# One decoder layer, one NeuronCore: token blocks of 264, or of 512, 512 and 32, instead of 352 in the merge's gate products

## The chip, the cores and the metric

The kernel runs on one core of a Trainium2 chip. The metric is the device time of one launch in microseconds. A core has TensorE (PE in the profile; PEld is its loading of weights), VectorE (DVE), ScalarE (ACT), GpSimd (POOL) and SyncE (SP, which only issues DMAs here). Each engine runs its own list of instructions in order, and waits on semaphores for the others.

## The reference, cut to what matters

One decoder layer for 1024 prompt tokens and 8 samples of 4 tokens, 1056 columns of 1024 features, all in float32:

```
u = x * (1 + scale1) + shift1
z = u @ w_in + b_in        # -> lru_in | lru_gate | s5_in | merge_gate_A | merge_gate_B, 1024 each
A = (RG-LRU(conv(lru_in)) * gelu(lru_gate)) @ w_lru_out
B = GLU(gelu(S5(s5_in)))   # 64 groups of 16 channels, a complex state of 64 each
mix = (sigmoid(merge_gate_A) * A + sigmoid(merge_gate_B) * B) @ w_out
x = LN(alpha * x + gate1 * mix);  x = LN(alpha * x + gate2 * SwiGLU(...))
```

The change is in the products for merge_gate_A and merge_gate_B, the last 2048 columns of w_in.

## The kernel before, in words

Features lie on the 128 partitions, tokens along the free dimension. A product takes one weight tile (1024 x 128, eight k tiles) against all 1056 tokens, and its tokens go in three blocks of 352, each into one of eight PSUM banks that are handed out in turn (`bank`). Weights and activations are each split into a high and a low part in float32r; a block is 8 k tiles x 3 combinations (high x high, high x low, low x high) = 24 matmuls of 128x128 weights on 352 columns, with a weight load for each (`mm`, L328). ACT makes the high part of the next weight tile (L216) and POOL the low part (L108) while the present one is used. The activations of w_in's products lie in `r1`: high or low, token block, k tile, 352 tokens. `make_u` writes them at the start.

The program is written out in one order for every engine. Each token block begins with a `tick`, and the S5's steps are noted against ticks (`S5_PLAN`, `s5_batch`), so that they land between blocks. The S5 goes in eight batches of groups, a new one every six ticks, which is two weight tiles of three blocks. Its steps on PE are the kernels (`s5_pe1`, L696), the transposes (`s5_pre4`, L706), the second stage, what each chunk adds to the states (`s5_pe2`, L734), and, for the batch before, the outputs (`s5_pe3`, L797 and L798), which need states that four DMAs copied (L784). They take 1, 2, 3 and 3 banks. DVE computes powers and rotations (L108), scans (L760) and gelu (L117), where the second gelu step (`s5_gelu2`) is the last reader of the outputs' banks. ACT copies results out of PSUM (L698 kernels, L708 transposes, L737 second stage, L800 squares of the outputs), takes the tanh for gelu (L807), prepares the scan's operands (L753, L755), and evacuates the products.

After the products of s5_in come 14 tiles for the merge's gates, eight for gate A and six for gate B, three ticks each; two more of gate B are done later, in the LRU stage. Their evacuation (L847) is a tanh on ACT into one staging buffer in the SBUF, which a DMA writes to DRAM when the tile is complete; the next tile's first evacuation waits for that DMA. Then the LRU stage begins.

Of the kernel before, what the change touches and what calls it, by code (L numbers as in the profile page):

```python
# [9 lines left out]
FT = mybir.dt.float32  # L10
# [5 lines left out]
T = 1056  # L16
# [10 lines left out]
# small operands, packed per partition: name, free shape  # L27
# [20 lines left out]
# float32 per partition  # L48
# [4 lines left out]
def _shaped(ap, shape):  # L53
    """[128, n] as [128, *shape]"""
    if len(shape) == 1:
        return ap
    names = "abcde"[:len(shape)]
    return ap.rearrange("p (" + " ".join(names) + ") -> p " + " ".join(names),
                        **dict(zip(names[1:], shape[1:])))
# [3 lines left out]
def tile_hawk_s5(ctx: ExitStack, tc: tile.TileContext, io):  # L63
# [3 lines left out]
    class Region:  # L67
        """a part of the SBUF; float32r where products read it"""
# [104 lines left out]
    r1r, r1f = acts(r1)  # L173
# [58 lines left out]
    # w_down's last part goes where the blocks of tokens have been read, one after another  # L232
# [34 lines left out]
    # w_out, and w_down's last part, stay whole: they go through the blocks of tokens  # L267
# [28 lines left out]
    def split_to(n):  # L296
        """splits of the tiles before the n-th, as far as the loads have come"""
# [14 lines left out]
    def use_w(name, m):  # L312
        """the next tile; the one after it is split meanwhile"""
# [9 lines left out]
    def mm(out, w, x, nb, kts, first=True, last=True):  # L323
        """out (+)= (hi + lo)^T (hi + lo) over k tiles, but for lo^T lo"""
# [14 lines left out]
    # =================== conditioning ===================  # L339
# [18 lines left out]
    # 2 silu(c)  # L358
# [19 lines left out]
    def ada_job():  # L378
        """two k tiles for four more tiles of the conditioning, beside the products, in the last bank"""
# [33 lines left out]
    # =================== S5 ===================  # L413
    s5m = {}

    def s5_open():
        """the S5's operands: in the right part, with the left part's help"""
# [35 lines left out]
    # exact exponentials, sines and cosines of small operands  # L453
    class Ops:
        """operations of DVE, noted down to run between others"""
# [7 lines left out]
        def turns(self, other):  # L463
            """the operations of both by turns"""
# [65 lines left out]
    def s5_small():  # L530
        """softplus(-lambda); the steps and abar, for pairs of groups and for rows of both parts"""
# [69 lines left out]
    def s5_powers():  # L601
        """abar^0..8; rows [re; im] and [-im; re]"""
# [30 lines left out]
    def s5_const1(b):  # L633
        """b abar^s and c abar^l, rows of real and of imaginary parts"""
# [30 lines left out]
    def s5_turn(ee, n0, n1):  # L665
        """e^{8 i theta (c + 1)} of the chunks c, by doubling"""
# [11 lines left out]
    def s5_turn0():  # L678
        """the first chunks, of all groups"""
# [10 lines left out]
    def s5_pe1(b):  # L690
        """the kernels c abar^l b, blocks of a Toeplitz matrix"""
# [8 lines left out]
    def s5_pre4(b):  # L700
        """b abar^s transposed"""
# [24 lines left out]
    def s5_pe2(b):  # L726
        """what each chunk adds to the states"""
# [11 lines left out]
    def s5_rot_in(b):  # L739
        """into the frame that turns with the states, where the recurrence is real"""  # L740
# [47 lines left out]
    def s5_pe3(b):  # L788
        """outputs, 2 gelu(y)"""
# [35 lines left out]
    def s5_last():  # L825
        """last states of the samples: abar^4 x0 + what the steps add"""
# [25 lines left out]
    # =================== program: z_s5, the merge's gates, S5 ===================  # L852
# [64 lines left out]
    for j in range(8):  # L917
        product(use_w("in", 24 + j), r1r, merge_evac(d_ta, j, 24 + j))
    for j in range(6):
        product(use_w("in", 32 + j), r1r, merge_evac(d_tb, j, 32 + j))  # L920

    # =================== program: LRU ===================
# [16 lines left out]
    # v, split, is kept where the last k tile goes  # L939
# [61 lines left out]
    def lru_0(j):  # L1001
        # t_c = tanh(log_a / 2), t_e = 1 + exp(log_a)
# [5 lines left out]
    def lru_1(j):  # L1008
        # t_d = 2 (1 + a) by a step of Newton's
# [561 lines left out]
```

## Time and profile before

| | |
|---|---|
| median of the 2 runs shown | 1877.1 us (1876.12 and 1878.08) |
| span of the profiled execution | 1876.2 us; the profile gives no other time of its own |
| PE busy | 1766.6 us (94%), 11640 matmuls |
| DVE busy | 974.8 us (52%) |
| ACT, POOL busy | 619.9 us (33%), 798.3 us (43%) |
| mean granted TensorE clock | 0.976 of full |

The gates' products run between about 156 and 385 us of the span. Busy shares of the whole span say little about that stretch: in its first two thirds DVE has hardly a gap, later PE has none. So it is read by stretches, and by what each engine waits for there. Times in the rows are microseconds from the span's start, then the duration; "x24" counts instructions, and brackets hold the idle time of the engine before a row with what ended it. Matmuls are pipelined, so a row of them ends with the last one's own duration.

### The profile page before, as it was taken

To read this page: it belongs to the slowest core of one execution; us is meant where nothing else is said; L and a number is where in the kernel's file an instruction comes from. 1 tells how busy PE (TensorE), PEld (TensorE's weight loads), DVE (VectorE), ACT (ScalarE), POOL (GpSimd) and SP (SyncE) were. 2 spreads that over 40 slices of the span, in tenths; PEclk is the share of its full clock that TensorE was granted. 3 is DMA by queue.
4 is the path that set the end of the run, shared out by engine and by line. 5 is a ranking of instruction groups with operands and counts; after the bars stand their busy time and mean duration, and the time that the engine had idled before them with its cause. 6 is when DMAs were issued, how large, how long until landed. Compare 5 with 4: busy or idle time off the path is not lost.

```text
span 1876.2 us, 28961 instructions
## 1 busy us (share of the span) xinstructions
PE 1766.6 (94%) x11640; PEld 1724.6 (92%) x11640; DVE 974.8 (52%) x1560; ACT 619.9 (33%) x1212; POOL 798.3 (43%) x663
## 2 busy tenths in 40 slices
PE   6899989899898899999999799999999999999994
PEld 5899988899788899999999799999999999999984
DVE  6989999648888743333248841231132112211297
ACT  4433333345554633212224552112211221122233
POOL 3557666427666622233342543223323332233435
PEclk9999999999899899999999999999999999999997
DMA  9334544431111158533351010111111111111111
GB/s 342 108 106 135 161 146 140 130 123 60 48 41 59 48 139 246 172 123 126 137 198 65 23 45 26 43 58 49 35 51 57 46 37 43 57 46 43 51 35 67
DMA packets 89846, 171.92 MB, mean 92 GB/s; under 512 B 18928, under 2 KB 54000, under 8 KB 89712
## 3 DMA queue, kind: packets, MB, share of 16 engines
q1 hardware_dynamic: 89712, 170.07, 28.1%
q8 instruction: 91, 1.49, 0.3%
q14 instruction: 43, 0.35, 0.1%
HBM read 136.86 MB, written 29.02 MB: 88 GB/s over the span
## 4 chain that ended last, share of the span: by engine, by line
PE 60%; DVE 19%; POOL 8%; issue 8%; ACT 3%; DMA 2%; SPq 0%; POOLq 0%; ACTq 0%; DVEq 0%
PE ps L328 57%; DVE s_t L108 8%; DVE norm_t L108 2%; POOL weights_t L108 2%; POOL lru_t L108 2%; DVE m_t L108 2%; POOL r_t L108 2%; DVE left_t L108 2%; DVE s_t L760 1%; DVE m_t L117 1%; PE ps L387 1%; DVE s_t L117 1%; POOL m_t L108 1%; DVE small_r_t L472 1%; DVE small_l_t L472 0%
## 5 line engine op out<-in xcount | busy, mean ns | idle before, releaser
L328 PE MATMUL ps<-r_t,weights_t 128*128 128x352 f32 x7632 | 1262.3, 326 | 2.2 <-ACT weights_t L216 1.1
L328 PEld LDWEIGHTS ps<-r_t,weights_t 128*128 128x128 f32 x7632 | 1236.7, 191 | 15.5 <-issue 8.9
L108 POOL TENSOR_TENSOR weights_t<-small_t,weights_t 128x512 fp32r<-128x512 f32 (+2 forms) x260 | 344.0, 1341 | 598.3 <-ACT weights_t L216 542.0
L216 ACT ACTIVATE weights_t<-small_t 128x512 fp32r<-128x512 f32 (+2 forms) x262 | 145.7, 599 | 257.1 <-PE ps L328 137.1
L328 PE MATMUL ps<-f_t,weights_t 128*128 128x352 f32 x1206 | 194.5, 322 | 0.0
L328 PEld LDWEIGHTS ps<-f_t,weights_t 128*128 128x128 f32 x1206 | 193.7, 188 | 0.0
L117 DVE SCALAR_TENSOR_TENSOR norm_t<-norm_t,ps 128x352 f32<-128x352 f32 x66 | 34.4, 521 | 222.4 <-ACT norm_t L1344 222.4
L108 DVE TENSOR_TENSOR s_t<-s_t 128x128 f32<-128x128 f32 (+3 forms) x200 | 134.4, 719 | 12.7 <-ACT s_t L737 7.0
L108 DVE TENSOR_TENSOR norm_t<-norm_t,ps 128x352 f32<-128x352 f32 x66 | 34.4, 521 | 195.8 <-PE ps L328 195.6
L117 DVE SCALAR_TENSOR_TENSOR m_t<-ps,small_t,m_t 128x352 f32<-128x352 f32 (+1 forms) x120 | 68.4, 570 | 126.9 <-PE ps L328 126.8
L108 POOL TENSOR_TENSOR f_t<-norm_t,f_t 128x352 fp32r<-128x352 f32 x66 | 62.7, 951 | 154.0 <-ACT f_t L1352 154.0
L117 DVE SCALAR_TENSOR_TENSOR glu_t<-glu_t,ps 128x352 f32<-128x352 f32 x48 | 24.2, 518 | 185.3 <-PE ps L328 126.3
L328 PE MATMUL ps<-r_t,f_t 128*128 128x352 f32 x648 | 107.1, 326 | 0.1
L328 PEld LDWEIGHTS ps<-r_t,f_t 128*128 128x128 f32 x648 | 105.0, 190 | 1.6 <-issue 0.5
L1352 ACT ACTIVATE f_t<-norm_t 128x352 fp32r<-128x352 f32 x66 | 32.8, 498 | 200.9 <-DVE norm_t L108 200.9
L117 DVE SCALAR_TENSOR_TENSOR lru_t<-lru_t 128x1056 f32<-128x1056 f32 (+1 forms) x52 | 81.9, 1574 | 30.6 <-ACT lru_t L998 16.6
L108 POOL TENSOR_TENSOR m_t<-m_t,norm_t 128x352 f32<-128x352 f32 x58 | 62.4, 1101 | 76.7 <-ACT norm_t L1206 64.8
L117 DVE SCALAR_TENSOR_TENSOR lru_t<-lru_t,small_t 128x352 f32<-128x352 f32 (+2 forms) x96 | 87.9, 916 | 3.4
L1344 ACT ACTIVATE norm_t<-ps 128x352 f32<-128x352 f32 x66 | 30.6, 464 | 177.1 <-PE ps L328 177.1
L108 POOL TENSOR_TENSOR left_t<-s_t 128x512 f32<-128x512 f32 (+1 forms) x40 | 77.0, 1947 | 5.8 <-DVE s_t L108 3.5
L328 PE MATMUL ps<-f_t,r_t 128*128 128x352 f32 x378 | 63.7, 327 | 0.9 <-POOL r_t L108 0.5
L328 PEld LDWEIGHTS ps<-f_t,r_t 128*128 128x128 f32 x378 | 61.0, 188 | 2.7 <-POOL r_t L108 0.8
(210 smaller groups left out, 1586.4 us busy)
## 6 DMA issues: line engine op xcount, KB each, us to landing
small_t<-in_w_up_dram SPq DMA_DIRECT2D x44, 512.0 KB
small_t<-in_w_in_dram SPq DMA_DIRECT2D x40, 512.0 KB
small_t<-in_w_ada_dram SPq DMA_DIRECT2D x32, 512.0 KB
ada_w_t<-in_w_ada_dram SPq DMA_DIRECT2D x16, 512.0 KB
small_t<-in_w_glu_dram SPq DMA_DIRECT2D x16, 512.0 KB
small_t<-in_w_down_dram SPq DMA_DIRECT2D x16, 384.0 KB
small_t<-in_w_down_dram SPq DMA_DIRECT2D x16, 320.0 KB
d_u<-left_t SPq DMA_DIRECT2D x64, 72.0 KB
```

Source lines behind the costliest of these rows:

```text
L108: e.tensor_tensor(out, a, b, op=op)
L117: e.scalar_tensor_tensor(out, a, s, b, op0=op0, op1=op1)
L216: A.activation(self.hi[:, s], self.raw[:, s], AF.Copy)
L328: PE.matmul(out[:, :NB], a[:, k, :], x[:, h, nb, k, :], start=bool(first and n == 0 and q == 0), stop=bool(last and n == len(kts) - 1 and ...
L387: PE.matmul(b[32 * j:32 * j + 32, :128], silu_c[:, 2 * i + k, :], w.raw[:, k, 128 * j:128 * j + 128], start=i == k == 0, stop=i == 3 and k ...
L472: getattr(V, name)(*a, **k)
L760: V.tensor_tensor_scan(wf[:, 512 * r:512 * r + 512], tv[:, :512], vv[:, r].rearrange("p n c -> p (n c)"), 0.0, op0=OP.mult, op1=OP.add)
L1344: A.activation(p, b[:, :NB], AF.Tanh, scale=0.5)
L1352: A.activation(frr[:, 0, nb, k, :], p, AF.Copy)
```

## The change

The two groups of gate products use a new helper, `product_wide`: the eight tiles of gate A go in four blocks of 264 tokens, the six tiles of gate B in blocks of 512, 512 and 32. Each tile keeps three ticks; a fourth block follows the third without one. So that a block may begin anywhere, `r1` now holds the tokens of a k tile as one row of 1056 (high or low, k tile, token); the other products see the same memory as three blocks of 352. The evacuation `merge_wide` takes any width. Comments and doc strings are gone from the changed file, and its lines have other numbers: L350 is the matmul of `product_wide`; L713, L723, L751, L814 and L815 are the former L696, L706, L734, L797 and L798; L330 is the former L328.

```diff
-    r1r, r1f = acts(r1)
+    r1r, r1f = (r1.v(0, 2, 8, 3, NB, t=t).rearrange("p h k n t -> p h n k t") for t in (FR, FT))
+    r1w = r1.v(0, 2, 8, T, t=FR)
...
+    def product_wide(w, x, widths, evac):
+        o = 0
+        for i, n in enumerate(widths):
+            if i < 3:
+                tick()
+            b = bank()
+            for k in range(8):
+                for q, (a, h) in enumerate(((w.hi, 0), (w.hi, 1), (w.lo, 0))):
+                    PE.matmul(b[:, :n], a[:, k, :], x[:, h, k, o:o + n], start=k == q == 0,
+                              stop=k == 7 and q == 2)
+            evac(o, n, b)
+            o += n
+        assert o == T
...
+    def merge_wide(d, j, m):
+        st = s5m["stage"]
+        def evac(o, n, b):
+            A.activation(st[:, o:o + n], b[:, :n], AF.Tanh, bias=bh[:, m - 24:m - 23], scale=0.5)
+            if o + n == T:
+                SP.dma_start(d[j], st)
+        return evac
...
     for j in range(8):
-        product(use_w("in", 24 + j), r1r, merge_evac(d_ta, j, 24 + j))
+        product_wide(use_w("in", 24 + j), r1w, (264,) * 4, merge_wide(d_ta, j, 24 + j))
     for j in range(6):
-        product(use_w("in", 32 + j), r1r, merge_evac(d_tb, j, 32 + j))
+        product_wide(use_w("in", 32 + j), r1w, (512, 512, 32), merge_wide(d_tb, j, 32 + j))
```

PE's list in a round of the S5 that falls on two tiles of gate A, from the kernels (L696, then L713) to the second stage (L734, then L751), with the semaphores that it waits for; r_t is r1. Before:

```order
L696 MATMUL ps<-s_t 32x128 [waits DVE_49,Activation_49]
L696 MATMUL ps<-s_t 32x128 x7
L328 MATMUL ps<-r_t,weights_t 128x352 [waits Activation_49]
L328 MATMUL ps<-r_t,weights_t 128x352 x23
L706 MATMUL ps<-small_t,s_t 128x128 [waits DVE_49,Pool_49]
L706 MATMUL ps<-small_t,s_t 128x128 x3
L706 MATMUL ps<-small_t,s_t 128x128 [waits DVE_49]
L706 MATMUL ps<-small_t,s_t 128x128 x3
L328 MATMUL ps<-r_t,weights_t 128x352 [waits DVE_49]
L328 MATMUL ps<-r_t,weights_t 128x352 x23
L734 MATMUL ps<-s_t 64x136 [waits DMAHW4_49,Activation_49]
```

The same round in the changed kernel:

```order
L713 MATMUL ps<-s_t 32x128 [waits DVE_49,Activation_49]
L713 MATMUL ps<-s_t 32x128 x7
L350 MATMUL ps<-r_t,weights_t 128x264 [waits DVE_49]
L350 MATMUL ps<-r_t,weights_t 128x264 x23
L723 MATMUL ps<-small_t,s_t 128x128 [waits DVE_49,Pool_49]
L723 MATMUL ps<-small_t,s_t 128x128 x3
L723 MATMUL ps<-small_t,s_t 128x128 [waits DVE_49]
L723 MATMUL ps<-small_t,s_t 128x128 x3
L350 MATMUL ps<-r_t,weights_t 128x264 [waits Activation_49]
L350 MATMUL ps<-r_t,weights_t 128x264 x23
...
L751 MATMUL ps<-s_t 64x136 [waits DMAHW4_49,Activation_49]
```

Two blocks instead of one stand between the transposes and the second stage. The block behind the kernels now waits for DVE, where it waited for ACT: it takes the first bank that the outputs of the batch before left, the one that the transposes took.

PE's list from the last batch's second stage to the first product of the LRU stage. Before:

```order
L734 MATMUL ps<-left_t,s_t 64x136 x16
L328 MATMUL ps<-r_t,weights_t 128x352 x24
L797 MATMUL ps<-s_t 128x136
L798 MATMUL ps<-s_t 128x136
...
L328 MATMUL ps<-r_t,weights_t 128x352 x144
L797 MATMUL ps<-left_t,s_t 128x136
L798 MATMUL ps<-s_t,left_t 128x136
...
L328 MATMUL ps<-r_t,weights_t 128x352 x192
```

And in the changed kernel:

```order
L751 MATMUL ps<-left_t,s_t 64x136 x16
L350 MATMUL ps<-r_t,weights_t 128x512 x24
...
L350 MATMUL ps<-r_t,weights_t 128x512 x24
L350 MATMUL ps<-r_t,weights_t 128x32 x24
L350 MATMUL ps<-r_t,weights_t 128x512 x48
L350 MATMUL ps<-r_t,weights_t 128x32 x24
L350 MATMUL ps<-r_t,weights_t 128x512 x24
L814 MATMUL ps<-left_t,s_t 128x136
...
L350 MATMUL ps<-r_t,weights_t 128x512 x24
L350 MATMUL ps<-r_t,weights_t 128x32 x24
L330 MATMUL ps<-r_t,weights_t 128x352 x144
```

One block stands between second stage and outputs of the batch before, as earlier; behind these, the six blocks of 352 have become four of 512 and two of 32. Of the 192 matmuls behind the last outputs, 48 were the gates'; they are now one block of 512 and one of 32.

## Rows read from the trace of the kernel before

**Rows 1.** The page, its first line.
```profile
span 1876.2 us, 28961 instructions
```

**Rows 2.** Windows: stretch, length, busy us per engine (instructions), granted clock, DMA.
```profile
280.00:348.50 68.50, 61.67 (x469) 59.25 (x467) 66.21 (x86) 23.71 (x61) 43.73 (x25) 1.00 0.45 140
348.50:371.40 22.90, 22.90 (x146) 22.90 (x146) 10.92 (x14) 9.05 (x22) 8.51 (x7) 1.00 0.40 112
```

**Rows 3.** Chain of waits, 90 to 420 us: shares by line; pieces (start, length).
```profile
by line: DVE s_t L108 38.8%; PE ps L328 20.4%; issue 9.8%; DVE s_t L760 6.9%; DVE left_t L108 6.8%; DVE s_t L117 4.1%; DMA s_t<-s_t 2.7%; PE ps L734 2.4%; PE ps L798 1.7%; PE ps L797 1.5%; ACT lru_t L998 0.9%; ACT s_t L684 0.5%; POOL left_t
...
345.01 0.23 PE ps L797 x2
...
364.18 2.44 DMA s_t<-s_t
...
371.29 2.45 DMA s_t<-s_t
```

**Rows 4.** Timeline of PE: a round of the S5 (start, length, line).
```profile
291.77 0.65 PE L696 MATMUL ps<-s_t 128*32 128x128 f32 x16
292.35 4.08 PE L328 MATMUL ps<-r_t,weights_t 128*128 128x352 f32 x24
297.69 1.07 PE L706 MATMUL ps<-small_t,s_t 128*128 128x128 f32 x8 [1.26 <-DVE s_t L117]
298.51 4.07 PE L328 MATMUL ps<-r_t,weights_t 128*128 128x352 f32 x24
304.72 2.10 PE L734 MATMUL ps<-s_t 128*64 128x136 f32 x32 [2.15 <-ACT s_t L708]
306.75 4.08 PE L328 MATMUL ps<-r_t,weights_t 128*128 128x352 f32 x24
...
314.29 11.70 PE L328 MATMUL ps<-r_t,weights_t 128*128 128x352 f32 x72
...
338.89 2.10 PE L734 MATMUL ps<-left_t,s_t 128*64 128x136 f32 x32 [2.13 <-ACT s_t L708]
```

**Rows 5.** Timeline of DVE in that round.
```profile
296.99 1.38 DVE L117 SCALAR_TENSOR_TENSOR s_t<-s_t,ps 128x408 f32<-128x408 f32 x3
...
303.50 6.92 DVE L108 TENSOR_TENSOR s_t<-s_t 128x64 f32<-128x64 f32 x18 [0.47 <-ACT s_t L684]
...
311.88 5.04 DVE L108 TENSOR_TENSOR s_t<-s_t 128x128 f32<-128x128 f32 x3
```

**Rows 6.** Timeline of ACT, that round and the end of the S5.
```profile
304.07 1.08 ACT L708 ACTIVATE s_t<-ps 128x512 f32<-128x512 f32 x2
...
306.50 1.23 ACT L737 ACTIVATE s_t<-ps 128x408 f32<-128x408 f32 x3
...
352.63 0.55 ACT L847 ACTIVATE left_t<-ps,small_t 128x352 f32<-128x352 f32 x1 [2.03 <-PE ps L328]
```

**Rows 7.** Timeline of PE, end of the S5.
```profile
348.46 23.14 PE L328 MATMUL ps<-r_t,weights_t 128*128 128x352 f32 x144
...
373.87 0.47 PE L798 MATMUL ps<-s_t,left_t 128*128 128x136 f32 x2 [1.57 <-DMA s_t<-s_t]
...
376.87 31.18 PE L328 MATMUL ps<-r_t,weights_t 128*128 128x352 f32 x192
```

**Rows 8.** Instructions on the banks: duration ns min/median/max, first and last start.
```profile
L328 PEld LDWEIGHTS ps<-r_t,weights_t x7632: 186/188/338, 15.5 to 1769.1; 128*128 128x128 f32 x196
L328 PE MATMUL ps<-r_t,weights_t x7632: 317/322/663, 15.5 to 1769.3; 128*128 128x352 f32 x196
...
L734 PEld LDWEIGHTS ps<-s_t x128: 133/137/230, 104.5 to 306.4; 128*64 128x64 f32 x128
```

**Rows 9.** Timeline of DVE: the last batch's scan.
```profile
355.23 2.34 DVE L760 TENSOR_TENSOR_SCAN s_t<-s_t 128x512 f32<-128x512 f32 x2 [2.65 <-POOL s_t L756]
```

**Rows 10.** Timeline of PE behind a longer wait, and that stretch's window.
```profile
167.94 3.90 PE L734 MATMUL ps<-s_t 128*64 128x136 f32 x32 [3.06 <-ACT s_t L708]
...
164.00:174.00 10.00, 6.94 (x46) 6.29 (x45) 9.30 (x23) 5.09 (x13) 3.88 (x3) 0.66 0.44 105
```

## The prediction

> **What bounds the kernel now.** I read the span first, then the busy time of each engine by stretch, then the chain of waits, and then the rows of PE, DVE and ACT through two rounds of the S5. The profiled execution spans 1876.2 us [rows 1], which is 0.9 below the median of the two runs shown, 1877.1. My sum is made against the span, and those 0.9 are added at the end.
>
> The stretch in which the gates' products run has two bounds, one after the other. From 280 to 348.5 us DVE is busy for 66.2 of 68.5 us and PE for 61.7; from 348.5 to 371.4 PE is busy all of the time and DVE for under half of it [rows 2]. The chain of waits from 90 to 420 us says the same: its largest share is DVE's S5 work and the products (L328) have 20% [rows 3]. The reader is to see that TensorE time added before about 340 us may be free, and that added later is not.
>
> In the first part a round of S5 (one batch of groups, two weight tiles) takes 34.2 us, from the second stage's matmuls at 304.72 to the next batch's at 338.89 [rows 4]. PE waits twice in it: 1.3 us before the transposes, for a DVE instruction that reads the bank they want, and 2.1 us before the second stage, for ACT's copy of the transposes. Both follow DVE's pace: DVE's second gelu instruction frees its first bank at 296.99 + 0.46 = 297.45, and its 18 rotations begin at 303.50 [rows 5], after which ACT copies the transposes from 304.07 to 305.15 [rows 6].
>
> **What one product costs.** Six blocks of 352, 144 matmuls, run without a gap from 348.46 for 23.14 us at full granted clock [rows 2, 7]; less the last one's own 0.32 [rows 8] that is 22.82 us for 143, 159.6 ns each. That clock is the 2.4 GHz level, so 352 columns are 146.7 ns and 12.9 ns are left over per matmul. A block of 24 is 3.83 us. I take the 12.9 as fixed, because each matmul brings one weight load whatever its width:
> - 264 columns: 110 + 12.9 = 122.9 ns, 2.95 us a block. A tile is 4 x 2.95 = 11.8 us against 3 x 3.83 = 11.5, 0.3 more.
> - 512 columns: 213.3 + 12.9 = 226.2 ns, 5.43 us a block. From below, the S5's f32 matmuls of 136 columns run at 0.23 us a pair [rows 3]; if a column takes them two cycles, that is 115 ns against 113.3, an excess near 2 ns, and makes 5.2. From above, in proportion to the columns, 159.6 x 512 / 352 = 232 ns makes 5.57. The middle is nearest, since it has the same operands and the same loads.
> - 32 columns: 13 ns of columns, so the load sets the pace. Loads of 128 columns last 188 ns and of 64 columns 137 [rows 8]; 51 / 64 = 0.8 ns a column, 102 ns for 128. The S5's pairs, each with its own load of 128, show that one in 115 ns can be kept. I take 110, 2.64 us a block. The upper end is 159.6, 3.83 us, as if narrowing saved nothing.
>
> A tile of 512, 512, 32 then costs 13.5 us against 11.5, 2.0 more, and six of them 12. The question is how much of it DVE's bound hides.
>
> **The eight tiles of 264.** They add 2 x 0.3 = 0.6 us to a round of two tiles. A round's PE work is now 6 x 3.83 = 23.0, plus kernels 0.57, transposes 0.82, second stage 2.03 and outputs 3.7 (314.29 - 306.75 less a block) [rows 4]: 30.1 of 34.2 us. It becomes 30.7, so 3.5 us stay idle. One order changes: with four blocks the eight banks come round one block sooner, and it is the block behind the kernels, not the transposes, that now waits for DVE's gelu. From 297.45 follow that block 2.95, transposes 0.82 and two blocks 5.9, which puts the second stage at 307.1 instead of 304.72. ACT's copies of its result ended 3.0 us after its start, at 307.73 [rows 6]; they now end near 310.1. DVE comes to its first possible reader of them at 311.88 [rows 5]. There are 1.8 us to spare, so DVE's pace stays and I cost these tiles at nothing. If that cover went, each round would be late by what is missing, next on DVE's rotations and then on ACT's queue.
>
> **The six tiles of 512, 512, 32.** They begin one block before the kernels at 291.77. From the gelu's release at 297.45 PE no longer waits. Up to the last batch's second stage come five blocks of 512 (27.15), three of 32 (7.92), twice the transposes (1.64), second stage 2.03, outputs 3.7 and kernels 0.57: 43.0 us, so 340.5 instead of 338.89, or **+1.6**. (ACT's copy, the old bound there, would have allowed about 339.2.) Behind it, before the last outputs, seven blocks of 352 (26.8) become five of 512 and two of 32 (32.4): **+5.6**. PE's wait of 1.57 us in the last outputs, for states that arrive by DMA at 373.7 [rows 3, 7], is eaten: **-1.6**. Those states will be later too, since ACT takes the second block's copy (352.63, on PE's end) ahead of the tanh and the scan's operands [rows 6], and DVE waits 2.65 us for these [rows 9]; that block ends about 4.3 us later. So the states land near 378, when PE arrives at 378.5, and they cost nothing more. The last two blocks, 7.66, become 8.07: **+0.4**. In all +6.0.
>
> The LRU stage opens on these products, and PE is on the path until it starts (192 matmuls in one run from 376.87 [rows 7]), so I expect the whole shift to stay. The order of k tile and token block in r1 changes no operand's count: ACT and POOL write the same 1056 elements per k tile, PE reads 352 contiguous columns as before. Eight more ACT evacuations and 0.15 us more for a wide one lie in ACT's slack. I cost these at nothing; if ACT were late, the states' copy and with it the rotations would be late.
>
> **Forecast**, 60%: 1876.2 + 6.0 + 0.9 = 1883. Its bounds: with blocks of 5.2 and 2.45 us, the eleven wide ones since 297.45 give back 2.5 and the six narrow ones 1.1, 1879.5; with 5.57 and 3.83 they add 1.5 and 7.1, 1892.
>
> **Rivals.**
> - The clock falls in the narrow blocks (20%), slower. PE streams for only 13 of 110 ns there, 2.6 us on end, in two of the six tiles right behind transposes of 0.8. After a wait of 3.06 us the clock went to the 1.2 GHz level: the second stage took 3.90 us instead of 2.10, and the granted clock was 0.66 over 10 us [rows 10]. That is 6.8 us at half, 3.4 us lost. The waits of 2.15 us brought no fall [rows 2, 4], and no row has a load-bound stream. All six narrow blocks lie on PE's path: one fall each makes 6.0 + 20.4, 1903.5; half of them 1893. It decides from about three falls on. The Trainium skill ("TensorE: Matmul & The Clock Gate", HAM oscillation) says that gaps in matmul work re-throttle the clock; whether a stream bound by loads counts as a gap, it does not say.
> - The narrow block costs next to nothing (8%). If 24 of them took 0.6 us, PE would be back at ACT's bound at 339, the seven blocks would be 28.4, and the last two 6.0 instead of 7.66; the states, late by the second block, would hold the last outputs by 3: about +1.4, 1878.5. Against it stand the loads' 102 to 115 ns. The Trainium skill (same page, Back-to-back issue gap) gives an issue floor of about 25 ns for 1 to 64 columns, by which this rival would come true; its section on LDWEIGHTS has 107 ns for 128 columns, and the trace agrees with that one.
> - The bank wait reaches DVE (7%), slower: where the clock falls in the 3.5 us that PE idles before the gelu's release, the second stage comes 3.4 us later than I have it, 1.6 more than the cover. Over four rounds that is +6, 1889.
> - The LRU stage takes the shift up (5%): 1877 to 1879. For that something other than PE would have to set when it starts; the rows show PE running into it without a gap [rows 7].
>
> So the range is 1876 to 1896; it leaves out the clock's worst third and mishaps on either side. Two per cent, 37.5 us, is about what a measurement of this kernel can tell from no change. No case here saves that much: the columns are the same and the loads not fewer, 1%. Slower by that would need the falling clock together with a late DVE, 3%. Within, 96%.
>
> **What would show it.** In the changed profile: matmuls of 512 columns at 226 ns and of 32 at 110; rounds of 34.2 us through the tiles of 264, with PE waiting some 3.5 us ahead of the block behind the kernels and DVE as busy as before; the last second stage near 340.5, the last outputs near 378.5 without a wait, and LRU's first product 6 us later. Wrong would be a granted clock under 1 between 300 and 390 us, narrow blocks well off 2.6 us, or rounds longer than 34.2.

## The result, and the profile after

The changed kernel takes 1886.46 us (median of 1884.69 and 1888.23) against 1877.1, a ratio of 1.0054, interval 1.0036 to 1.0072. The forecast was 1883.0, the range 1876 to 1896. Its profiled execution took 1888.23 us, 1.8 more than its span, where the forecast had put 0.9 around the span of before; with the same 1.8, the profiled execution of before was the slower of the two shown, 1878.08. In what follows a "fall" is a stretch that the record of TensorE's clock has at the 1.2 GHz level (a granted clock of about 0.5 in a window).

The page's first line, to be held against [rows 1]:

```profile
span 1886.4 us, 29354 instructions
```

The windows of the changed kernel, with the columns of [rows 2] (stretch, length, busy us of PE, PEld, DVE, ACT and POOL, granted clock, DMA):

```profile
280.00:348.50 68.50, 68.16 (x453) 59.16 (x453) 61.97 (x86) 24.41 (x61) 43.17 (x25) 0.95 0.47 139
348.50:384.00 35.50, 35.50 (x189) 30.43 (x188) 12.14 (x15) 9.49 (x22) 10.45 (x8) 0.95 0.38 108
339.50:342.70 3.20, 3.20 (x35) 3.17 (x34) 2.79 (x10) 1.40 (x5) 0.00 (x0) 1.00 0.44 81
342.70:346.10 3.40, 3.40 (x29) 3.04 (x26) 0.00 (x0) 2.30 (x5) 2.49 (x2) 0.51 0.76 161
```

Two things differ from [rows 2]. PE is busy for 68.2 of 68.5 us before 348.5 where it was busy for 61.7, and DVE has gone from 66.2 to 62.0: the bound has passed to PE some 40 us earlier than before (PE's last wait there ends at 296.37, in the rows below, and at 338.89 in [rows 4]). And the mean clock is 0.95 where it was 1.00. The last two rows show why: through a narrow block and up to its end (339.5 to 342.7) the clock is full, and in the 3.4 us behind it half. The chain of waits from 90 to 420 us says the same of the bound: products of the new form (L350) lead it, where DVE's L108 led in [rows 3].

```profile
by line: PE ps L350 29.9%; DVE s_t L108 25.0%; PE ps L330 14.1%; issue 6.0%; DVE left_t L108 5.2%; DVE s_t L777 4.6%; PE ps L751 3.8%; DVE s_t L117 3.1%; PE ps L815 2.8%; PE ps L814 2.8%; PE ps L723 1.1%; PE ps L713 0.7%; ACT s_t L701 0.3%;
```

PE's timeline, with the columns of [rows 4] (L713, L723 and L751 are the kernels, the transposes and the second stage, L696, L706 and L734 before; outputs are left out):

```profile
193.41 5.65 PE L350 MATMUL ps<-r_t,weights_t 128*128 128x264 f32 x24 [4.48 <-DVE s_t L117]
...
205.89 2.07 PE L751 MATMUL ps<-left_t,s_t 128*64 128x136 f32 x32
...
262.39 3.20 PE L350 MATMUL ps<-r_t,weights_t 128*128 128x264 f32 x24 [2.98 <-DVE s_t L117]
...
296.37 5.84 PE L350 MATMUL ps<-r_t,weights_t 128*128 128x512 f32 x24 [0.34 <-DVE s_t L117]
302.05 1.04 PE L723 MATMUL ps<-small_t,s_t 128*128 128x128 f32 x8
302.84 2.83 PE L350 MATMUL ps<-r_t,weights_t 128*128 128x32 f32 x24
305.60 2.07 PE L751 MATMUL ps<-s_t 128*64 128x136 f32 x32
307.61 5.83 PE L350 MATMUL ps<-r_t,weights_t 128*128 128x512 f32 x24
...
316.89 15.61 PE L350 MATMUL ps<-r_t,weights_t 128*128 128x512 f32 x72
...
339.48 2.83 PE L350 MATMUL ps<-r_t,weights_t 128*128 128x32 f32 x24
342.24 3.46 PE L751 MATMUL ps<-left_t,s_t 128*64 128x136 f32 x32
345.63 6.06 PE L350 MATMUL ps<-r_t,weights_t 128*128 128x512 f32 x24
...
355.15 29.40 PE L350 MATMUL ps<-r_t,weights_t 128*128 128x512 f32 x144
...
388.01 8.39 PE L350 MATMUL ps<-r_t,weights_t 128*128 128x512 f32 x48
```

At 193.41 and 262.39 PE waits 4.48 and 2.98 us ahead of the block behind the kernels, for the bank that DVE's gelu still reads, as forecast for the tiles of 264; behind the 0.34 us at 296.37 it waits for nothing. The second stage takes 2.07 us at 305.60 and 3.46 at 342.24, right behind a narrow block. From the latter to the last outputs at 384.4 stand 42.2 us, where before it was 32.5 (338.89 to 371.4). Some 1.7 us of that are only moved: 2624 tokens of the products stand in this time where 2464 did, and so many fewer behind it (24 x 160 x 0.444 ns, the pace found in e7); and in the last outputs there is no longer the wait of 1.57 us [rows 7]. Falls begin at 325.7, 342.7, 363.2 and 397.4 us and last 3.4 us each. Each begins within 1.3 us of the start of a narrow block's last matmul (325.0, 342.0, 363.3 and 396.1), so at the ends of four of the six narrow blocks. PE stood idle ahead of none of them. An earlier one, from 192.6 on for 6.8 us, begins in the wait of 4.48 us. The late second stage behind it (205.89) held DVE, whose timeline shows two waits there:

```profile
208.70 3.94 DVE L108 TENSOR_TENSOR s_t<-s_t 128x512 f32<-128x512 f32 x2 [2.00 <-ACT s_t L754]
214.86 4.48 DVE L108 TENSOR_TENSOR s_t<-left_t,s_t 128x1152 f32<-128x1152 f32 x2 [2.22 <-PE ps L815]
```

The pace, as the median from start to start in this trace: 112 ns for 32 tokens, 121 for 264, 160 for 352 and 232 for 512.

The shift against the trace of before is +13.0 us at the last outputs (371.4 to 384.4), +12.9 at the first matmul of the LRU stage's gates (412.5 to 425.4) and +10.2 at the end. From that matmul to the end the run of before took 1463.7 us and the ten profiled runs of the changed kernel (two) and of e1 to e5, e7, e9 and e10 below 1459.2 to 1462.2, so the missing 2.7 us seem to be that one run's (1878.08 us, where the same kernel's median beside e8 is 1875.66) and nothing that the LRU stage took up; in that later pairing the medians differ by 11.3.

### The profile page after: what moved, and what is told of

It is laid out like the page before. It is cut to its first block, busy times and chain, and to the rows that moved or that the text cites. A ratio compares the mean times of both kernels' runs of the same rounds, so it can differ in the third digit from the quotient of the medians.

```text
span 1886.4 us, 29354 instructions
## 1 busy us (share of the span) xinstructions
PE 1784.5 (95%) x11832; PEld 1731.3 (92%) x11832; DVE 968.0 (51%) x1560; ACT 623.6 (33%) x1220; POOL 800.1 (42%) x663
## 4 chain that ended last, share of the span: by engine, by line
PE 67%; DVE 14%; POOL 7%; issue 6%; ACT 3%; DMA 2%; SPq 1%; POOLq 0%; ACTq 0%; DVEq 0%
PE ps L330 58%; PE ps L350 5%; DVE s_t L108 5%; POOL weights_t L108 2%; DVE norm_t L108 2%; POOL lru_t L108 2%; POOL r_t L108 2%; DVE m_t L108 1%; DVE left_t L108 1%; DMA x_in_t<-in_x_dram 1%; DVE s_t L777 1%; PE ps L404 1%; DVE m_t L117 1%; PE ps L751 1%; DMA ada_w_t<-in_w_ada_dram 1%
## 5 line engine op out<-in xcount | busy, mean ns | idle before, releaser
L330 PE MATMUL ps<-r_t,weights_t 128*128 128x352 f32 x6624 | 1093.7, 326 | 1.9 <-ACT weights_t L218 1.1
L330 PEld LDWEIGHTS ps<-r_t,weights_t 128*128 128x128 f32 x6624 | 1074.7, 191 | 12.4 <-issue 6.7
L108 POOL TENSOR_TENSOR weights_t<-small_t,weights_t 128x512 fp32r<-128x512 f32 (+2 forms) x260 | 343.9, 1341 | 609.8 <-ACT weights_t L218 581.4
L350 PE MATMUL ps<-r_t,weights_t 128*128 128x264 f32 (+2 forms) x1200 | 188.4, 316 | 9.1 <-DVE s_t L117 9.1
L330 PE MATMUL ps<-f_t,weights_t 128*128 128x352 f32 x1206 | 194.5, 322 | 0.0
L330 PEld LDWEIGHTS ps<-f_t,weights_t 128*128 128x128 f32 x1206 | 193.8, 188 | 0.0
L350 PEld LDWEIGHTS ps<-r_t,weights_t 128*128 128x128 f32 x1200 | 169.2, 194 | 24.7 <-DVE s_t L117 10.2
L108 DVE TENSOR_TENSOR s_t<-s_t 128x128 f32<-128x128 f32 (+3 forms) x200 | 127.0, 683 | 17.6 <-ACT s_t L754 11.9
L108 DVE TENSOR_TENSOR norm_t<-norm_t,ps 128x352 f32<-128x352 f32 x66 | 34.4, 521 | 195.2 <-PE ps L330 195.0
L117 DVE SCALAR_TENSOR_TENSOR m_t<-ps,small_t,m_t 128x352 f32<-128x352 f32 (+1 forms) x120 | 68.4, 570 | 126.9 <-PE ps L330 126.8
L108 POOL TENSOR_TENSOR f_t<-norm_t,f_t 128x352 fp32r<-128x352 f32 x66 | 62.8, 951 | 153.3 <-ACT f_t L1378 153.3
L330 PE MATMUL ps<-r_t,f_t 128*128 128x352 f32 x648 | 106.5, 325 | 0.0
L330 PEld LDWEIGHTS ps<-r_t,f_t 128*128 128x128 f32 x648 | 104.7, 190 | 1.1 <-issue 0.5
L108 POOL TENSOR_TENSOR m_t<-m_t,norm_t 128x352 f32<-128x352 f32 x58 | 62.2, 1097 | 76.1 <-ACT norm_t L1232 65.0
L108 POOL TENSOR_TENSOR left_t<-s_t 128x512 f32<-128x512 f32 (+1 forms) x40 | 78.8, 1991 | 4.5 <-DVE s_t L777 2.3
```

Of the source, the lines that this page charges most:

```text
L108: e.tensor_tensor(out, a, b, op=op)
L117: e.scalar_tensor_tensor(out, a, s, b, op0=op0, op1=op1)
L330: PE.matmul(out[:, :NB], a[:, k, :], x[:, h, nb, k, :], start=bool(first and n == 0 and q == 0), stop=bool(last and n == len(kts) - 1 and ...
L350: PE.matmul(b[:, :n], a[:, k, :], x[:, h, k, o:o + n], start=k == q == 0, stop=k == 7 and q == 2)
```

## The experiments

My theory was: a narrow block costs the loads of 24 weights, and its end the falling clock; the first rival was that something else of the change (the 264 tiles, the layout, the 512 blocks, their evacuation) has a part in it. The kernel before ran again beside each group of these runs, with medians from 1875.27 to 1876.21 us, and each ratio is to the median beside it. The table gathers what they gave. "r6 to outputs" is the time in the profiled run from the second stage of round 6 (305.6 us in the changed kernel) to the last round's outputs (384.4), and the falls are those within it. Where gate B's blocks are 512 or 480 wide, 160 or 128 more tokens stand in that time and so many fewer behind it; these 1.7 or 1.4 us are no loss. In e3 they and one fall make most of the 3.7 us over the kernel before, and at the end nothing is lost.

| kernel | gate A | gate B | us | ratio [interval] | r6 to outputs, falls |
|---|---|---|---|---|---|
| before | 3 x 352 | 3 x 352 | 1877.1 | | 66.7, 0 |
| e1 | 4 x 264 | 3 x 352 | 1874.67 | 0.9990 [0.9982, 0.9999] | 67.1, 0 |
| e2 | 3 x 352 | 512, 512, 32 | 1886.16 | 1.0053 [1.0039, 1.0066] | 75.7, 1 |
| e3 | 4 x 264 | 512, 272, 272 | 1875.05 | 0.9992 [0.9984, 1.0001] | 70.4, 1 |
| e4 | 4 x 264 | 512, 512, 32 spread | 1882.14 | 1.0037 [1.0023, 1.0050] | 74.1, 0 |
| e5 | 3 x 352 | 3 x 352, new layout | 1875.87 | 1.0003 [0.9994, 1.0012] | 68.4, 2 |
| e8 | 4 x 264 | 512, 512, 32 (the change) | 1886.94 | 1.0062 [1.0050, 1.0075] | 78.9, 3 |
| e9 | 4 x 264 | 512, 512, 32 filled | 1881.73 | 1.0033 [1.0021, 1.0046] | 74.1, 0 |
| e10 | 4 x 264 | 480, 480, 96 | 1878.54 | 1.0018 [1.0009, 1.0027] | 71.1, 0 |
| e6 | 512, 512, 32 | 4 x 264 | 1891.70 | 1.0088 [1.0074, 1.0101] | |
| e11 | 512, 512, 32 filled | 4 x 264 | 1883.19 | 1.0041 [1.0028, 1.0053] | |
| e12 | as e11, banks moved on | 4 x 264 | 1878.03 | 1.0007 [0.9998, 1.0016] | |

### e1, e2: each gate's part alone

```diff
 e1: gate B as before, gate A as in the change
-        product_wide(use_w("in", 32 + j), r1w, (512, 512, 32), merge_wide(d_tb, j, 32 + j))
+        product(use_w("in", 32 + j), r1r, merge_evac(d_tb, j, 32 + j))
 e2: gate A as before, gate B as in the change
-        product_wide(use_w("in", 24 + j), r1w, (264,) * 4, merge_wide(d_ta, j, 24 + j))
+        product(use_w("in", 24 + j), r1r, merge_evac(d_ta, j, 24 + j))
```

> Gate A's eight tiles in four blocks of 264, gate B's six in three of 352 as before. Theory (DVE sets the pace of the S5's rounds, so PE time there is free): rounds of 34.2 us, LRU's first product within 1 us of before, total 1877 (1875.5 to 1878.5). Rival (the four blocks' bank wait, with a falling clock, reaches DVE and is part of the 9.4 us): last second stage 2 us or more later than 338.9, total 1880 or more.

> Gate A's tiles in blocks of 352 as before, gate B's in 512, 512 and 32. Theory (the whole loss comes from gate B's tiles): total 1885 to 1888, four or so falls of the granted clock between 300 and 400 us. Rival (264 is a part of it): 1880 to 1884.

The tiles of 264 alone cost nothing (1874.67). Gate B's alone give the loss: 1886.16 is 10.0 over the kernel before, and the interval overlaps with that of the changed kernel again (e8, 11.3 over). Some four falls were expected; the profile of e2, its quickest run with 1881.23 us, shows a single one, behind the narrow block that ends at 338.6:

```profile
338.50:342.50 4.00, 4.00 (x35) 3.61 (x35) 3.93 (x7) 2.51 (x6) 2.81 (x2) 0.57 0.40 75
```

```profile
335.88 2.83 PE L350 MATMUL ps<-r_t,weights_t 128*128 128x32 f32 x24
338.64 3.54 PE L751 MATMUL ps<-left_t,s_t 128*64 128x136 f32 x32
...
351.56 27.86 PE L350 MATMUL ps<-r_t,weights_t 128*128 128x512 f32 x144
```

Six blocks from 351.56 (four of 512, two of 32) take 27.86 us here at full clock, and 29.40 in the changed kernel, which has one fall in them. So the number of falls changes from run to run. That the slower runs of e2 (1884.30 to 1887.59) had more of them at this place is not shown, since they have no trace; their mean granted clocks, 0.969 to 0.973 against 0.977, fit it.

### e3, e4: without the narrow block, and with it spread out

```diff
 e3
-        product_wide(use_w("in", 32 + j), r1w, (512, 512, 32), merge_wide(d_tb, j, 32 + j))
+        product_wide(use_w("in", 32 + j), r1w, (512, 272, 272), merge_wide(d_tb, j, 32 + j))
 e4: the last half of the second block, for n = 0 to 11
+            step(1, 12 + n)      # 512 tokens
+            step(2, 2 * n)       # 32 tokens
+            step(2, 2 * n + 1)   # 32 tokens
```

> Gate B's blocks are 512, 272 and 272 instead of 512, 512 and 32: the same number of matmuls and loads, no block so narrow that loads set its pace. Theory (the narrow block is the whole cause, by its loads and by the clock behind it): 232 ns and about 124 ns a matmul, 11.5 us a tile, no fall of the clock between 300 and 400 us, total 1877 to 1879. Rival (blocks of 512, that fill a bank and have a long evacuation, cost time of their own): half of the loss stays, 1881 or more.

> The same matmuls as the change, but the 24 narrow ones stand two by two between the last twelve of the second 512 block, so that no stretch of PE's list is bound by loads for long; the S5's steps keep their places, the second block's evacuation moves behind the third tick. Theory (about half of the loss is the clock, which falls behind a narrow block): no fall between 300 and 400 us, total 1878 to 1881, of which up to 1 us a tile may come from loads that hide behind the wide matmuls. Rival (only the loads cost, the falls are chance): 1885 to 1888 with falls, or without them no gain.

Without narrow blocks nothing is lost (e3), so the blocks of 512 are not to blame. The expectation of no fall was wrong there: one begins at 339.7, behind a wait of PE ahead of the last second stage.

```profile
338.74 3.10 PE L751 MATMUL ps<-left_t,s_t 128*64 128x136 f32 x32 [2.89 <-ACT s_t L725]
```

In e4 one 512 and two 32 take 453 ns together (starts at 303.27, 303.73 and 304.18), and apart they would be 232 + 2 x 112 = 456: spreading hides no load, though the two narrow ones start 27 ns apart. The time, 1882.14, lies 1 us over the range expected. But no fall is left between 300 and 400 us:

```profile
280.00:348.50 68.50, 68.17 (x470) 59.35 (x469) 63.07 (x87) 24.27 (x62) 44.27 (x26) 1.00 0.46 136
348.50:384.00 35.50, 35.50 (x212) 31.11 (x210) 11.08 (x17) 10.88 (x25) 7.71 (x7) 1.00 0.44 134
```

The ratio is 1.0037 where the change has 1.0062 (e8), 4.7 us less. That points to the clock for these and leaves 6 us for the loads; the intervals only just touch, and e9 below asks the same in another way.

### e5: the layout alone

```diff
-        product_wide(use_w("in", 24 + j), r1w, (264,) * 4, merge_wide(d_ta, j, 24 + j))
+        product(use_w("in", 24 + j), r1r, merge_evac(d_ta, j, 24 + j))
 ... and gate B as in e1
```

> The first activations lie in the new order, k tile by k tile, and all fourteen tiles of both gates are multiplied in blocks of 352 tokens as before. Theory (the layout costs and saves nothing, the loss is the narrow blocks'): ratio 0.998 to 1.001, 1873 to 1878 us, outputs of the last round from about 371 us on, no fall of the granted clock between 300 and 400 us, 160 ns per 352 tokens. Rival (part of the loss is the layout's, because a strided or contiguous right-hand side changes the pace of the products): the 352-token products pass at another pace than 160 ns, and the run is over 1880 us.

The layout costs nothing, 160 ns per 352 tokens as before. The expectation of no fall was wrong: five rounds have one each, behind PE's wait of 2 us for ACT, which had brought none in the trace of before [rows 4].

```profile
304.42 3.12 PE L751 MATMUL ps<-s_t 128*64 128x136 f32 x32 [1.93 <-ACT s_t L725]
```

```profile
305.00:309.00 4.00, 4.00 (x32) 3.64 (x31) 3.93 (x7) 2.58 (x6) 2.80 (x2) 0.57 0.35 65
```

Those before 310 us cost nothing: the second stages stay 34.2 us apart (270.2, 304.4, 338.6), since DVE sets the pace there. The one at 339.5 lies where PE is the bound, and the last outputs begin 1.4 us later than before (372.9 against 371.4). In these traces a fall is paid only where PE is the bound.

### e6: the gates' widths swapped

```diff
-        product_wide(use_w("in", 24 + j), r1w, (264,) * 4, merge_wide(d_ta, j, 24 + j))
+        product_wide(use_w("in", 24 + j), r1w, (512, 512, 32), merge_wide(d_ta, j, 24 + j))
-        product_wide(use_w("in", 32 + j), r1w, (512, 512, 32), merge_wide(d_tb, j, 32 + j))
+        product_wide(use_w("in", 32 + j), r1w, (264,) * 4, merge_wide(d_tb, j, 32 + j))
```

> Gate A's eight tiles take 512, 512 and 32 tokens and gate B's six take 264: the narrow blocks now stand in rounds 0 to 7, where VectorE and not TensorE sets the pace. Theory (a narrow block costs 2.8 us of loads, and 1.7 us more where the clock falls, but only where TensorE has no idle time to give): a round of gate A takes TensorE up to 4.5 us more, of which the idle 3 to 4.5 us ahead of the block behind the kernels' matmuls gives back most; the last outputs begin 0 to 5 us later than before, and the whole is 1875 to 1882 us. Rival (the loss goes with the number of narrow blocks, wherever they stand): eight blocks instead of six, 1886 to 1891 us, last outputs begin 12 us or more later than before. Rival (a falling clock in narrow blocks also slows the second stage's and the kernels' matmuls, so that VectorE waits for TensorE): VectorE's scans fall behind by over 1 us a round.

The theory failed on the size: 1891.7, the worst of all, where it had 1875 to 1882. The timeline of PE, narrow blocks and the second stage behind them:

```profile
165.19 2.83 PE L350 MATMUL ps<-r_t,weights_t 128*128 128x32 f32 x24
167.96 3.40 PE L751 MATMUL ps<-s_t 128*64 128x136 f32 x32
...
203.43 2.88 PE L350 MATMUL ps<-r_t,weights_t 128*128 128x32 f32 x24
206.24 3.64 PE L751 MATMUL ps<-left_t,s_t 128*64 128x136 f32 x32
...
242.87 3.22 PE L751 MATMUL ps<-s_t 128*64 128x136 f32 x32
...
281.11 3.74 PE L751 MATMUL ps<-left_t,s_t 128*64 128x136 f32 x32
```

Every one of these second stages is slow (3.2 to 3.7 us against 2.07): six of the eight narrow blocks end in a fall. From second stage to second stage the rounds take 38.3, 36.6 and 38.2 us, with two, one and two falls, so about 35 us and 1.6 for each fall, where DVE's bound is 34.2 [rows 4]. PE's idle time in these rounds was eaten by loads and clock together, and DVE waits for PE. By these numbers the rivals came nearer than the theory, the one that counts narrow blocks wherever they stand (1886 to 1891) and the one that has DVE wait; e11 and e12 decide between them. The last outputs begin only 11.5 us later than before (382.9 against 371.4), while the median is 16 us later. Some 5 us are lost 600 us further on, which only e11 made plain.

### e7: one tile of each width

```diff
+    WIDTHS = ((480, 480, 96), (448, 448, 160), (416, 416, 224), (384, 384, 288), (496, 496, 64), (464, 464, 128))
-        product_wide(use_w("in", 32 + j), r1w, (512, 512, 32), merge_wide(d_tb, j, 32 + j))
+        product_wide(use_w("in", 32 + j), r1w, WIDTHS[j], merge_wide(d_tb, j, 32 + j))
```

> Gate B's six tiles take (480, 480, 96), (448, 448, 160), (416, 416, 224), (384, 384, 288), (496, 496, 64) and (464, 464, 128) tokens: one look at the pace of each width. Theory (a matmul waits for the load of its own weights, about 111 ns, and above that its time is in proportion to its tokens, 0.444 ns a token and 3.5 ns): 32 to 224 tokens take 111 to 113 ns whatever their number up to about 240 and then rise, 288 takes 131 to 132 ns, 384 174 ns, 416 188 ns, 448 203 ns, 480 217 ns, 496 224 ns. Rival (a fixed excess of 13 ns over a column per cycle): 384 takes 173 ns, 448 199.7 ns, 480 213 ns. On the clock: if the clock falls because TensorE does little in a block bound by loads, blocks of 160 and 224 tokens keep the full clock and those of 64 and 96 may lose it; if it falls because of the weight loads themselves, all narrow blocks lose it alike.

```profile
302.58 2.86 PE L350 MATMUL ps<-r_t,weights_t 128*128 128x96 f32 x24
...
307.37 5.12 PE L350 MATMUL ps<-r_t,weights_t 128*128 128x448 f32 x24
...
334.24 2.92 PE L350 MATMUL ps<-r_t,weights_t 128*128 128x224 f32 x24
```

| tokens | 32 (e8) | 64 | 96 | 128 | 160 | 224 | 264 | 288 | 384 | 416 | 448 | 464 | 480 | 496 | 512 (e8) |
|---|---|---|---|---|---|---|---|---|---|---|---|---|---|---|---|
| ns | 112 | 112 | 112 | 112 | 111 | 112 | 121 | 133 | 175 | 190 | 202.5 | 209.5 | 219 | 225 | 232 |

Up to 224 tokens the time does not depend on the width: the load decides, 111 to 112 ns. Above it the time grows in proportion: 480 tokens at 219 ns fit 0.444 ns a token and 3.5 (217) and not a column per cycle and 13 (213). This profile has no fall between 200 and 475 us, so behind none of its five blocks that are bound by loads (64, 96, 128, 160 and 224 tokens, one of each). The time is one run's, 1875.18.

### e8: the changed kernel again

> The changed kernel again, beside the others on the same chip. Theory (2.8 us of loads for each narrow block plus about 1.7 us for each fall of the clock, whose number differs from run to run): 1884 to 1888 us, with three to five falls of 3.4 us between 300 and 400 us in the profiled run, and a last round of outputs that begins 8 us later than before plus 1.7 us for each fall. Rival (the falls are a property of the one run shown, and the shift is the loads' alone): no fall, and the outputs begin 12 us later all the same.

```profile
303.49 2.85 PE L350 MATMUL ps<-r_t,weights_t 128*128 128x32 f32 x24
306.27 3.67 PE L751 MATMUL ps<-s_t 128*64 128x136 f32 x32
...
340.19 2.83 PE L350 MATMUL ps<-r_t,weights_t 128*128 128x32 f32 x24
342.95 3.21 PE L751 MATMUL ps<-left_t,s_t 128*64 128x136 f32 x32
```

Three falls between 300 and 400 us, at 306.2, 343.7 and 364.2, again at narrow blocks' ends: the first, third and fourth, where the first profile had the second, third, fourth and sixth. From the second stage of round 6 to the last outputs it is 78.9 us, and was 78.8 in the first profile. With 74.1 and no fall (e4, e9), 75.7 and one (e2), 78.8 and 78.9 and three, a fall is 1.6 us: 3.4 us at half clock.

### e9: narrow blocks that multiply 224 tokens and keep 32

```diff
+            f = 192 if n == 32 else 0
-                    PE.matmul(b[:, :n], a[:, k, :], x[:, h, k, o:o + n], ...
+                    PE.matmul(b[:, :f + n], a[:, k, :], x[:, h, k, o - f:o + n], ...
-            evac(o, n, b)
+            evac(o, n, b[:, f:])
```

> The narrow blocks of the changed kernel multiply the last 224 tokens and not the last 32; of the result only the last 32 columns are read, so 192 columns of each such block are computed twice. Number of matmuls, weight loads, blocks of 512 and reads of the banks stay; 224 tokens take 112 ns (seen in the run with many widths), as 32 do, so TensorE spends the same time on loads but streams columns nearly all of it. Theory (of the 10 to 12 us lost, about 4 to 5 are the clock's, which falls because TensorE streams for a small part of a load-bound block): no fall of the granted clock at the blocks' ends, 3.4 to 6 us faster than the changed kernel, 1881 to 1883 us, 74 us from the second stage of round 6 to the last outputs. Rival (the clock falls because of the stream of weight loads itself, whatever is multiplied): falls as before, 1886 to 1887 us, 77 to 79 us. Rival (the falls do not matter for the end of the program): no falls, but 1886 us all the same.

```profile
342.00:345.50 3.50, 3.50 (x40) 3.06 (x40) 0.93 (x4) 2.41 (x6) 2.45 (x2) 1.00 0.48 98
```

```profile
339.15 2.92 PE L351 MATMUL ps<-r_t,weights_t 128*128 128x224 f32 x24
342.00 2.07 PE L752 MATMUL ps<-left_t,s_t 128*64 128x136 f32 x32
...
353.29 27.86 PE L351 MATMUL ps<-r_t,weights_t 128*128 128x512 f32 x144
```

The same loads and the same blocks, seven times the columns in the narrow ones, and the block takes 2.92 us against 2.83 (112 ns from start to start in both). The clock stays full behind it, the second stage is back at 2.07, and the kernel is at 1.0033 where the change is at 1.0062. The loads are the same in both kernels, so they alone do not lower the clock; the two differ in the columns that the narrow blocks multiply. Both rivals fall.

### e10: 480, 480 and 96 in all of gate B

```diff
-        product_wide(use_w("in", 32 + j), r1w, (512, 512, 32), merge_wide(d_tb, j, 32 + j))
+        product_wide(use_w("in", 32 + j), r1w, (480, 480, 96), merge_wide(d_tb, j, 32 + j))
```

> All six tiles of gate B take 480, 480 and 96 tokens; 96 tokens take 112 ns and 480 219 ns, so that a tile costs 24 x (219 + 219 + 112) ns = 13.2 us, against 13.8 with 512, 512 and 32 and 11.5 with three times 352. Theory (loads by the widths, and falls that cost 1.7 us each): without any fall 4 to 5 us over the time before, 1880 to 1881 us; with as many falls as in the changed kernel 1884 to 1885 us. The run with many widths showed no fall at its one block of 96, so I expect the first. Rival (a narrow block costs the same whatever its width): 1886 us.

```profile
336.99 2.86 PE L350 MATMUL ps<-r_t,weights_t 128*128 128x96 f32 x24
339.78 2.07 PE L751 MATMUL ps<-left_t,s_t 128*64 128x136 f32 x32
...
350.73 26.55 PE L350 MATMUL ps<-r_t,weights_t 128*128 128x480 f32 x144
```

No fall at any of six blocks of 96, and 1878.54, 1.5 us under the expected range: of the 10 us that six tiles add by the widths, more is hidden than I had put. The last second stage comes only 0.9 us later than before (339.8), the last outputs 5.7 (377.1, with 1.4 of it moved tokens), and at the LRU stage's gates 3.7 are left (416.2 against 412.5).

### e11, e12: swapped and filled, and the banks

```diff
 e11: e6 with e9's narrow blocks; e12: e11 and, where eight banks go round again,
     banks[0] = 8
+    bank_at[0] += 2
```

> Gate A's tiles take 512, 512 and 32 tokens and gate B's 264, as in the run with the gates swapped, and the narrow blocks multiply 224 tokens of which 32 are read. In the swapped run a round of the S5 took 34.9 us plus 1.7 us for each fall of the clock in it (36.7 with one, 38.2 with two). Theory (the clock is what made those rounds longer than VectorE's 34.2): rounds of 34.2 to 35.0 us, no falls at the blocks' ends, last outputs 2 to 5 us later than before, 1877 to 1881 us. Rival (the loads alone make the rounds longer): 36 to 38 us a round and 1889 us or more.

> As the run with the gates swapped and the narrow blocks filled, but at the end of the modulation's matmuls, where the banks go round by eight again, the count of the banks is moved on by two, so that each later block gets the bank that it has in the changed kernel: with the gates swapped 48 blocks are counted in the gates' products, with the change 50. Both swapped runs had a wait of PE of 3.5 to 4.0 us near 975 us for DVE's reading of the modulation's bank, with a fall of the clock behind it, that no other run had, and were 5 to 7 us later from there on. Theory (that wait is the bank's, which the block behind the modulation's last matmul happens to get): no wait and no fall between 960 and 985 us, last outputs as in the run before near 375 us, 1876.5 to 1879 us. Rival (the wait comes with the gates' order through something else): it stays, and 1883 us as before.

With filled blocks the rounds are 35.1 us (203.9, 239.0 and 274.1 in e11), 0.1 over what was expected, without falls at the narrow blocks' ends (e11 has one at 332.8, behind a wait of 3.35 us in gate B's tiles); the last outputs begin at 375.1, as expected. Yet the median, 1883.19, is over the 1877 to 1881 expected. Going through later products one by one, e6 and e11 lose 5 and 7 us against e9 in one place, behind the last matmuls of the modulation (L415). PE's timeline there, of e6 (where L415 is L414), of e11 and then of e12:

```profile
977.53 0.30 PE L414 MATMUL ps<-small_t 128*128 128x36 f32 x2
981.31 5.46 PE L330 MATMUL ps<-r_t,weights_t 128*128 128x352 f32 x24 [3.48 <-DVE small_t L117]
```

```profile
971.35 0.30 PE L415 MATMUL ps<-small_t 128*128 128x36 f32 x2
975.69 6.62 PE L330 MATMUL ps<-r_t,weights_t 128*128 128x352 f32 x24 [4.04 <-DVE small_t L117]
```

```profile
966.68 0.30 PE L415 MATMUL ps<-small_t 128*128 128x36 f32 x2
966.82 4.06 PE L330 MATMUL ps<-r_t,weights_t 128*128 128x352 f32 x24
```

In e6 and e11 the next product waits 3.48 and 4.04 us for DVE's reading of a bank and then runs partly at half clock (5.46 and 6.62 us for a block of 4.06). Swapped, the gates' products are 48 blocks instead of 50, so that every later block gets another bank. Moving the count on by two takes the wait away; the last outputs begin at 372.2, earlier than expected (the fall at 332.8 is missing too), and 1878.03 us stand where 1883.19 were. The changed kernel's count is 50 and that of before 42: both leave the same remainder by eight, so neither has this wait. The rival of another cause is out.

## Why the prediction was right, and where it was not

- **Bound and place.** Right: TensorE time is free in the DVE-bound rounds and paid behind them. e1 (264 alone) is at 0.9990, and e12 (eight narrow blocks' loads in DVE's rounds, full clock) at 1.0007, where six in gate B cost 1.0033 (e9). It is not free without limit: e12's rounds take 35.1 us and not 34.2.
- **The tiles of 264.** Right: 121 ns (forecast 122.9), waits of 1.3 to 4.5 us ahead of the block behind the kernels (3.5 forecast). One of these, 4.48 us, came with a fall of 6.8 us, and the next second stage was 3.8 us later than before (205.9 against 202.1). So the rival of the bank wait did come, once, and the cover of 1.8 us did not hold: DVE waited 2.00 and 2.22 us. But its rotations ahead of that had taken 4.75 us where they took 6.93 before, and it came to its next gelu step only 0.3 us later (222.7 against 222.5). At 305.6 the second stage is 0.9 later, and e1, with waits of up to 4.47 us, loses nothing.
- **Widths.** The narrow block was right, 112 ns (110). The wide one was mis-sized: I held the excess of 12.9 ns to be fixed, and it is in proportion, 232 ns as by my upper bound. From the second stage of round 6 to the last outputs that is 9 blocks at 0.14 us, 1.3 us.
- **The sum of +6.0.** Right by the medians for a kernel whose clock stays full: e9, which keeps every load and block and has no fall there, is 6.5 us over before (1881.73 and 1875.27; ratio 1.0021 to 1.0046). The eaten wait and the last outputs without one came as written. Other terms were short: in e9's trace the last second stage begins at 342.0 (forecast 340.5), the last outputs at 381.0 (378.5), and the LRU stage's gates 7.9 us later than before (420.4 against 412.5). That is the slowest of e9's five runs, so how far short stays open; that 6.5 stands so near to 6.0 is in part luck.
- **The clock.** This is the step that failed. I gave it 20% and left it out of the sum, because no row had a load-bound stream and waits of 2.15 us had brought no fall. It came in four of six blocks, each for 3.4 us and not the 6.8 of [rows 10], so 1.6 us a fall instead of 3.4. That the time still lies inside the range is luck in this: four falls at the prediction's own 3.4 us would have made it 1896.6. By the medians it is worth 11.3 (e8) less 6.5 (e9), 4.8 us, three falls at 1.6. The Trainium skill ("TensorE: Matmul & The Clock Gate", HAM oscillation) tells of falls behind gaps in which the matmuls wait for data. These runs show falls with no gap at all, behind blocks of 32 columns that are bound by loads.
- **The nearly free narrow block.** Wrong, as expected. With a load for each matmul the traces show 112 ns for 32 and for 64 columns. The Trainium skill (same page, Back-to-back issue gap) has an issue floor of about 25 ns up to 64 columns. In e4 the two matmuls of 32 in a group start 27 ns apart, near that floor, but the group takes 453 ns, as if each paid its load. By the formula in the Trainium skill's section on LDWEIGHTS (same page) a load of 128 columns takes about 107 ns, an estimate (128 / 1.2), and the 112 ns agree with that one.
- **The shift stays.** Right: +13.0 at the last outputs, +12.9 at the LRU's gates; no stage behind took it up.
- **What can be told apart.** The prediction put it at two per cent. The interval of the two runs is 0.18 per cent to either side and those of five and more are narrower, so the 0.5 per cent lost here can be told from no change.

What stays open: why a given narrow block ends in a fall and another of the same form does not (four of six, three of six, one of six in three profiles), and at which width the falls end: 64 tokens were tried in one block only.

## What to carry to other kernels

Cutting this product's tokens unevenly bought nothing (512, 272 and 272 at 0.9992; 480, 480 and 96 at 1.0018; 512, 512 and 32 at 1.0062). Where every matmul loads its own weights, a block pays for the load up to some 240 tokens (an estimate: there 0.444 ns a token and 3.5 ns reach the 112 ns of the load), so narrower blocks are to be avoided; a third (352) and a quarter (264) of 1056 tokens are wide enough. Blocks of 32 tokens also brought a lower clock behind them, which is paid where TensorE is the bound. Multiplying 192 more columns and throwing them away took no more time there and kept the clock. And when a variant changes the number of blocks by other than a multiple of eight, look for a new wait far behind the change, since each later block gets another bank.

## What the runs showed of the hardware

- Weight-load-bound blocks of 32 tokens, 2.7 us long and without idle time, were followed by half clock for 3.4 us in 4, 3 and 1 of 6 cases (the first profile, e8, e2) and in 6 of 8 (e6); blocks of 96 (six, e10) and of 224 (six in e9, eight each in e11 and e12) in none.
- The pace of these matmuls is 111 to 112 ns from 32 to 224 tokens and 0.444 ns a token and 3.5 ns, within 2.5 ns, from 264 to 512.
- The same wait of 2 us ahead of the second stage brought no fall in the rounds of [rows 4] and one in each of five rounds of e5.
